# A hybrid decoder block on one core: the opening rebuilt with constant products in its waits, one w_in turn moved, the second norm with one root

## The chip, the core and the metric

The kernel runs on one core of a Trainium2 chip. The metric is the device time of one execution, in microseconds (us). The engines are named as in the profile: PE (matrix products), PEld (its weight loads, which overlap PE), DVE (vector), ACT (scalar), POOL (GpSimd) and SP, whose queue issues nearly all loads here.

## The reference

One decoder block, batch 1, 256 tokens, D = 2048, everything fp32. Cut to what matters:

```python
mod = silu(c) @ w_ada + b_ada                       # c: (1, 2048), w_ada: 2048 x 12288
sh1, sc1, g1, sh2, sc2, g2 = split(mod, 6)
h = rms_norm(x, norm1_g) * (1 + sc1) + sh1
q, k, v, gb, gc, xt = split(h @ w_in, 6)            # w_in: 2048 x 6144
attn = moba_attention(norm(q), norm(k), v)          # 256 tokens: one block, causal
conv = gb * causal_dwconv(gc * xt)
x = x + g1 * (concat(norm(attn), norm(conv)) @ w_out)
h2 = rms_norm(x, norm2_g) * (1 + sc2) + sh2
u_gate, u_up = split(causal_dwconv(h2 @ w_ffn_up), 2)
x = x + g2 * ((silu(u_gate) * u_up) @ w_ffn_down)
```

All inputs are drawn at random; `c` is one row, so each part of `mod` is one vector of 2048 numbers.

## The kernel before

**Precision.** An fp32 product is built from fp32r products of split operands: `hi` is the rounded copy of a weight tile (ACT, L329), `lo` the rest (DVE subtraction, L166, the line of the helper that records all DVE work), and likewise `h` and its residual for the tokens. A product is hi x h, lo x h and hi x residual of h, all into one PSUM bank.

**Slots.** The weights go by in slots: a raw tile of 1 MB is loaded (SP), split into hi on ACT, into lo on DVE, and multiplied on PE. There are six raw buffers (one of them holds partial sums for a while), three hi and three lo. The slots of w_in come in the order of the table `turns`: `['v', 2, 4]` is the pair of column groups v0, v1 on contraction chunks 2 and 3, one slot; `['g1', 4, 8]` is one group on four chunks, one slot. Slot 0 is c, 1 v, 2 g, 3 x, 4 and 5 q, 6 c, 7 and 8 k, 9 g, 10 to 12 x, 13 v; slot 24 is the last slot of `['q0', 4, 16]`. Partial sums leave PSUM when the next slot of the same columns is far: the first time by a copy on ACT (L531), later by an addition on DVE (L166), tiles `pa_...`.

**Banks.** PSUM has eight banks, and `bank()` hands out the one that has been free longest. A slot with a pair takes four (two column groups by two tiles of 128 tokens). Two groups fill the eight; an ada part on PE (below) takes one between them. So slot 3 (x) gets three banks that held v, and as its fourth the first one of g: the first product into it waits for the first eviction of g on ACT, which stands in ACT's queue behind the hi of slot 4.

**adaLN parts ("ada").** `mod` is needed column by column. A part is either multiplied on PE (`pe` true: four column quadrants, weights `crep`, which is silu(c) copied 32 times; L396), or added up on DVE with one scalar_tensor_tensor a chunk (L387, L389). Each part then takes a transpose and a reduction to become columns (`cols`, L453). The table `ada` says [part, first chunk, width, pe, first slot, number of slots over which its tiles are spread]; its tiles share the load queue with the slots. `[1, 4, 512, False, 3, 7]` is the scale for chunks 4 to 7, four tiles.

**Order.** Each engine works through its own list in order; the lists follow from the order in which the Python code, `turns`, `ada` and lists such as `x_first` and `hi_late` emit instructions. Loads are issued on SP in the order in which the tiles are consumed.

**The opening** (L1479 to L1565): x is transposed in 128x128 pieces (L1495, xn) while the sum of squares runs on ACT; the root of the first norm becomes two diagonal tiles n1d, which PE multiplies with ones (n1b, L1509) to get the root along the free axis; xnT = xn times that, on DVE. Beside it run the first ada parts on PE: scale for chunks 0 and 1 (two tiles of 1 MB), then shift. Each is copied out (adae, ACT L417), transposed (adac, L453) and reduced on DVE (adaz). The scaled tokens hf, the shift and the hi of slot 0 give the first product mc (`go_first`, L583: 16 products with hi, 8 with lo).

**The second norm** (`evac_c`, `diag`, L700 to L736): the last w_out column group is added to x, its squares are summed, and the two token tiles get their roots one after the other; n2d, n2b and h2 follow as in the first norm, and the first slots of w_up (`one`, L1042 to L1050) multiply the first h2.

Of the kernel before, what the change touches and what calls it, by code (L numbers as in the profile page):

```python
# [147 lines left out]
def tile_block(  # L148
# [77 lines left out]
    V.tensor_copy(identb, ident)  # L226

# [118 lines left out]
    class Ada:  # L346


        def __init__(self, part, c0, n, pe):
            self.part, self.c0, self.n, self.pe = part, c0, n, pe  # L350
            self.rows = 2048 // n
            self.tiles = NK // self.rows
            self.nch = n // P
            self.acc = None
            self.two = []
            self.used = 0

        def want(self, r):
            a = self.part * D + self.c0 * P
            k0 = r * self.rows  # L360

            def issue(t):
                nc.sync.dma_start(self.view(t), w_ada[0, k0 * P:(k0 + self.rows) * P, a:a + self.n]
                                  .rearrange("(k p) f -> p k f", p=P))
            return issue

# [172 lines left out]
    def pair_load(k, f):  # L539
        def issue(t):  # L540

            n = 1 if not slots_begun else 2
            slots_begun.append(f)
            for j in range(0, 2, n):
                nc.sync.dma_start(t.rearrange("p (k h) f -> p k (h f)", k=2)[:, j:j + n],
                                  w_in[0, (k + j) * P:(k + j + n) * P, COL[f] * 512:COL[f] * 512 + 1024]
                                  .rearrange("(k p) f -> p k f", p=P))
# [152 lines left out]
    def evac_c(f):  # L700
# [7 lines left out]
        def one(t, s, i):  # L708
            V.scalar_tensor_tensor(out=y[t][:, s], in0=g[i][:, :s.stop - s.start], scalar=r[:, t:t + 1], in1=gB[G1, f][:, s],
                                   op0=ALU.mult, op1=ALU.mult)  # L710
            if i == 2:

                V.scalar_tensor_tensor(out=ss2[:, 3, 1:2], in0=q[:, 1:2], scalar=1.0 / D, in1=ss2[:, 3, 1:2],
                                       op0=ALU.mult, op1=ALU.add)
# [316 lines left out]
    def up_slots(grp, ka, kb, one, hold, between=None):  # L1031
        for k in range(ka, kb, 4):
            def go(hi, lo, k=k):
# [9 lines left out]
                if one:  # L1043
                    for j in range(4):
                        for ft in range(4):
                            o, a = zp[grp][ft][:, :256], slice(ft * P, (ft + 1) * P)
                            for w, v in ((hi, 0), (hi, 1), (lo, 0)):
                                mm(o, w[:, j, a], h2T[k + j][:, v * 256:v * 256 + 256],  # L1048
                                   start=begins and j == 0 and w is hi and not v,
                                   stop=ends and j == 3 and w is lo)  # L1050
# [120 lines left out]
    ada_init = [Ada(SC1, 0, 256, True), Ada(SH1, 0, 256, True)]  # L1171

# [331 lines left out]
    ada_init[0].consume(0)  # L1504
    pr = bank("n1b")
# [25 lines left out]

# [3 lines left out]
    parts = [(slice(2 * k, 2 * k + 2), t1k("hf"), t2k(f"h{k}", F32R)) for k in range(2)]  # L1535
    b1 = SH1 * NK
    for k, (s, h, hk) in enumerate(parts):
        hT[k] = halves(hk)
        V.tensor_scalar(h, xnT[0][:, k * 256:(k + 1) * 256], A1[:, k:k + 1], bcol[:, b1 + k:b1 + k + 1],
                        op0=ALU.mult, op1=ALU.add)  # L1540
    s = parts[0][0]
    if CFG["first_hi"]:
        V.tensor_copy(hi[:, s], w[:, s])
    else:
        act(hi[:, s], w[:, s], AF.Copy)
    z, _ = ada_init[1].cols(True)
    for k, (s, h, hk) in enumerate(parts):
        act(hT[k][0], h, AF.Identity, bias=z[:, k:k + 1])
        if not k:
            act(hi[:, parts[1][0]], w[:, parts[1][0]], AF.Copy)  # L1550
    for k, (s, h, hk) in enumerate(parts):
        V.scalar_tensor_tensor(out=hT[k][1], in0=h, scalar=z[:, k:k + 1], in1=hT[k][0].bitcast(F32),
# [106 lines left out]
```

## Time and profile before

| what | us |
|---|---|
| three runs | 1145.74, 1145.96, 1147.56; median 1145.96 |
| the profiled execution | 1145.98 |
| its span (first to last instruction) | 1144.2 |
| PE busy in the span | 1129.7 (99%) |
| DVE busy | 1064.4 (93%) |
| ACT busy | 731.6 (64%) |
| waits of PE for another engine or a load, sum | about 10.8, nearly all before 24 us |

The mean TensorE clock granted in the profiled execution is 0.997 of full speed. A row of the timeline reads: start, duration of the group, engine, line, operation, out<-in, shape, count, and in brackets the idle time of the engine before it with what ended it. A row of the table by windows reads: window, its length, busy time and number of instructions of PE, PEld, DVE, ACT and POOL, then the granted PE clock, the busy share of the DMA engines and the GB/s.

### The profile page before, as it was taken

How to read it: one execution, taken by the hardware profiler on the slowest of the kernel's cores; microseconds unless marked ns; L12 is line 12 of the kernel's file. 1: busy time of each engine (PE TensorE's matmuls, PEld its weight loads, DVE VectorE, ACT ScalarE, POOL GpSimd, SP SyncE). 2: the span in 40 equal slices, each digit the busy share in tenths (PEclk: the TensorE clock that was granted, in tenths of full speed). 3: DMA queues.
4: the chain of work that ended last, by engine and by line, in shares of the span. 5: the costliest groups of instructions: out<-in, count | busy, mean ns of one | idle time of the engine just before them, and what ended most of it. 6: DMA issues, size and time to landing. Idle time of an engine off the chain costs nothing.

```text
span 1144.2 us, 16252 instructions
## 1 busy us (share of the span) xinstructions
PE 1129.7 (99%) x6035; PEld 954.1 (83%) x6035; DVE 1064.4 (93%) x1167; ACT 731.6 (64%) x1091; POOL 61.5 (5%) x90
## 2 busy tenths in 40 slices
PE   6999999999999999999999999999999999999998
PEld 4777778888888879988888888888888888888887
DVE  4789989989999998889999999899999999999798
ACT  4644455576786555566687676776677768866731
POOL 1000000000000000000000000101011101111000
PEclk8999999999999999999999999999999999999999
DMA  9999998998998899987679887999899988999951
GB/s 361 407 412 397 412 371 302 408 382 308 331 397 314 290 317 359 325 278 245 213 246 369 305 293 248 310 360 299 313 272 340 317 317 265 351 313 303 367 222 74
DMA packets 198687, 363.66 MB, mean 318 GB/s; under 512 B 9408, under 2 KB 108180, under 8 KB 194000
## 3 DMA queue, kind: packets, MB, share of 16 engines
q1 hardware_dynamic: 189152, 343.44, 82.8%
q0 software_dynamic: 8160, 17.04, 6.9%
q10 hardware_dynamic: 1296, 2.16, 0.6%
q8 instruction: 47, 0.77, 0.2%
q14 instruction: 32, 0.26, 0.1%
HBM read 343.70 MB, written 18.89 MB: 317 GB/s over the span
## 4 chain that ended last, share of the span: by engine, by line
PE 94%; DVE 2%; DMA 2%; issue 1%; ACT 1%; SPq 0%; DVEq 0%; ACTq 0%
PE z L1063 24%; PE z L1066 13%; PE u L1002 4%; PE u L1004 4%; PE u L1000 4%; PE z L1048 4%; PE ada L396 1%; DVE lo L166 1%; PE mx L516 1%; PE mq L516 1%; PE mg L516 1%; PE mk L516 1%; PE mx L517 1%; PE mv L516 1%; PE mg L517 1%; PE mq L517 1%
## 5 line engine op out<-in xcount | busy, mean ns | idle before, releaser
L329 ACT ACTIVATE hi<-raw 128x2048 fp32r<-128x2048 f32 (+1 forms) x227 | 417.6, 1857 | 263.6 <-DMA raw<-in_w_in_dram 73.5
L166 DVE TENSOR_TENSOR lo<-raw,hi 128x2048 fp32r<-128x2048 f32 (+2 forms) x229 | 501.6, 2200 | 23.3 <-ACT hi L329 23.1
L1063 PE MATMUL z<-h,hi 128*128 128x512 f32 x1280 | 303.3, 390 | 0.3 <-DVE ub L166 0.3
L1063 PEld LDWEIGHTS z<-h,hi 128*128 128x128 f32 x1280 | 237.8, 188 | 49.5 <-ACT hi L329 0.8
L389 DVE SCALAR_TENSOR_TENSOR ada<-raw,csil,ada 128x512 f32<-128x512 f32 (+3 forms) x167 | 195.7, 1175 | 5.3 <-DMA raw<-in_w_ada_dram 1.8
L1066 PEld LDWEIGHTS z<-h,lo 128*128 128x128 f32 x1280 | 163.1, 191 | 5.6
L1066 PE MATMUL z<-h,lo 128*128 128x256 f32 x1280 | 165.0, 283 | 0.0
L1002 PE MATMUL u<-hi,gh 128*128 128x512 f32 x224 | 88.1, 394 | 0.1
L1004 PE MATMUL u<-hi,gl 128*128 128x512 f32 x224 | 87.7, 392 | 0.0
L1000 PE MATMUL u<-lo,gh 128*128 128x512 f32 x224 | 61.4, 390 | 0.0
L812 ACT ACTIVATE uy<-ub,fc,fc 128x256 f32<-128x256 f32 x88 | 47.6, 599 | 11.9 <-DVE ub L166 11.9
L944 POOL DMA_DIRECT2D down_sums<-pu x42 | 36.7, 1290 | 304.3 <-ACT pu L940 304.3
L1002 PEld LDWEIGHTS u<-hi,gh 128*128 128x128 f32 x224 | 42.2, 188 | 10.0 <-ACT pu L940 2.9
L1000 PEld LDWEIGHTS u<-lo,gh 128*128 128x128 f32 x224 | 41.9, 188 | 9.2 <-DVE lo L166 0.3
L1004 PEld LDWEIGHTS u<-hi,gl 128*128 128x128 f32 x224 | 42.2, 189 | 7.5
L1048 PE MATMUL z<-h,hi 128*128 128x256 f32 x256 | 46.6, 284 | 0.4 <-ACT h L771 0.2
L823 ACT ACTIVATE tap<-ub,fc 128x256 f32<-128x256 f32 x96 | 41.7, 504 | 0.0
L1048 PEld LDWEIGHTS z<-h,hi 128*128 128x128 f32 x256 | 40.0, 192 | 0.8 <-ACT h L771 0.5
L166 DVE TENSOR_TENSOR ub<-z,ub 128x256 f32<-128x256 f32 x96 | 33.8, 414 | 7.2 <-ACT ub L844 7.1
L301 DVE TENSOR_TENSOR raw<-raw 128x1024 f32<-128x1024 f32 x32 | 38.9, 1217 | 1.2 <-DMA raw<-in_w_ffn_down_dram 1.2
L844 ACT ACTIVATE ub<-z 128x256 f32<-128x256 f32 x96 | 28.6, 383 | 12.7 <-PE z L1063 12.7
L1048 PE MATMUL z<-h,lo 128*128 128x256 f32 x128 | 36.2, 283 | 0.0
(460 smaller groups left out, 1787.3 us busy)
## 6 DMA issues: line engine op xcount, KB each, us to landing
raw<-in_w_ada_dram SPq DMA_DIRECT2D x96, 1024.0 KB, 7.4
raw<-in_w_ffn_up_dram SPq DMA_DIRECT2D x176, 512.0 KB, 6.1
raw<-in_w_in_dram SPq DMA_DIRECT2D x47, 1024.0 KB, 8.1
raw<-in_w_ffn_down_dram SPq DMA_DIRECT2D x44, 1024.0 KB, 9.5
raw<-in_w_out_dram SPq DMA_DIRECT2D x16, 1024.0 KB, 5.9
raw<-in_w_ffn_down_dram SPq DMA_DIRECT2D x32, 512.0 KB, 4.9
down_sums<-pu POOLq DMA_DIRECT2D x56, 256.0 KB, 8.0
raw<-in_w_ffn_down_dram SPq DMA_DIRECT2D x32, 256.0 KB, 5.3
```

Source lines behind the costliest of these rows:

```text
L166: f(*a, **k)
L329: act(hi[:, :n], t[:, :n], AF.Copy)
L389: W.scalar_tensor_tensor(out=self.acc, in0=t[:, j, :], scalar=csil[:, i:i + 1], in1=self.acc, op0=ALU.mult, op1=ALU.add)
L516: mm(o, a, hi[:, k, s], start=(first and k == 0), stop=False)
L812: act(y[:, s], b[:, s], AF.Identity, bias=bias[:, i + j:i + j + 1], scale=w[2][:, i + j:i + j + 1])
L823: act(z[:, s], b[:, s], AF.Copy, scale=w[2 - d][:, i + j:i + j + 1])
L1000: mm(bank_of(key), a, lo[:, n], start=False, stop=j in ends)
L1002: mm(bank_of(key), a, hi[:, n], start=key not in begun, stop=False)
L1004: mm(bank_of(key), b, hi[:, n], start=False, stop=False)
L1048: mm(o, w[:, j, a], h2T[k + j][:, v * 256:v * 256 + 256], start=begins and j == 0 and w is hi and not v, stop=ends and j == 3 and w is lo)
L1063: mm(zp[grp][ft], hi[:, j, ft * P:(ft + 1) * P], h2T[k + j], start=begins and j == 0, stop=ends and j == 3 and not late)
L1066: mm(zp[grp][ft][:, :256], lo[:, j, ft * P:(ft + 1) * P], h2T[k + j][:, :256], start=False, stop=ends and j == 3 and late)
```

## The change

Five pieces, all in one step.

1. The opening. 34 constant products `onesr` x `onesr` (128x128, result used by nobody) stand between the real PE work. The second shift tile is loaded and multiplied in two halves. The shift's columns come from two products with a 128x1 column `sel` in place of two transposes and a reduction. hf moves ahead on DVE; the first h is made on DVE and the second on ACT; slot 0's load is four DMAs of 128x512, and its hi four pieces, two on ACT and two on DVE.
2. `turns`: v on chunks 2 and 3 goes from slot 13 to slot 7, in front of k; k1, v0, g1 follow each other in a new order.
3. `ada`: the scale for chunks 4 to 7 starts two slots later and is spread over six slots instead of seven.
4. The second norm: the mean squares of both token tiles, one root for both, then both diagonals.
5. The `one` slots of w_up: for each chunk first hi x h for four row tiles, then lo x h, then hi x residual; before, the three came row tile by row tile. `x_first` and `hi_late`, which shift pieces of FFN work by a place, change in some entries.

```diff
-  ..., [1, 4, 512, False, 3, 7], ...
+  ..., [1, 4, 512, False, 5, 6], ...
-       'turns': [['c', 0, 2], ['v', 0, 2], ['g', 0, 2], ['x', 0, 2], ['q', 0, 2], ['q', 2, 4], ['c', 2, 4], ['k', 0, 4],
-                 ['g', 2, 4], ['x', 2, 4], ['x', 4, 8], ['v', 2, 4], ['g1', 4, 8], ['k1', 4, 8], ['v0', 4, 8], ['c', 4, 8],
+       'turns': [['c', 0, 2], ['v', 0, 2], ['g', 0, 2], ['x', 0, 2], ['q', 0, 2], ['q', 2, 4], ['c', 2, 4], ['v', 2, 4],
+                 ['k', 0, 4], ['g', 2, 4], ['x', 2, 4], ['x', 4, 8], ['k1', 4, 8], ['v0', 4, 8], ['g1', 4, 8], ['c', 4, 8],
+       'busy': [9, 4, 5, 5, 5, 6],
+       'norm_at': [4, 8, 8],
...
+    V.tensor_reduce(out=sel, in_=ident.rearrange("p (j r) -> p j r", j=4)[:, :, 0], axis=AX.X, op=ALU.add)
...
+    def keep_busy(b, n):
+        for _ in range(n):
+            mm(b[:, 256:384], onesr, onesr, start=True, stop=True)
...
-    xn_norm(0, 1, 2, 3)
-    ada_init[0].consume(1)
-    ada_init[0].evac()
-    ada_init[0].cols()
-    xn_norm(4)
+    xn_norm(*range(n0))
+    sc.consume(1)
+    keep_busy(p_one, w1)
+    sc.evac()
+    sc.cols()
+    hf = []
+    b1 = SH1 * NK
+    for k in range(2):
+        hf.append(t1k("hf"))
+        V.tensor_scalar(hf[k], xnT[0][:, k * 256:(k + 1) * 256], A1[:, k:k + 1], bcol[:, b1 + k:b1 + k + 1],
+                        op0=ALU.mult, op1=ALU.add)
+    xn_norm(*range(n0, 5))
     xn_tr(5)
-    ada_init[1].consume(0)
+    keep_busy(p_one, w2)
+    sh.products(0, 0, 8)
     xn_tr(6, 7)
-    xn_norm(5, 6, 7)
-    ada_init[1].consume(1)
-    ada_init[1].evac()
+    keep_busy(p_one, w3)
+    xn_norm(*range(5, n1))
+    sh.products(1, 0, 4)
+    sh.products(1, 4, 8)
+    keep_busy(p_one, w4)
+    rows_sum = t2k("adae")[:, :256]
+    act(rows_sum, sh.acc, AF.Copy)
+    for k in range(2):
+        mm(p_one[:, k:k + 1], rows_sum[:, k * P:(k + 1) * P], sel, start=k == 0, stop=k == 1)
+    keep_busy(bank("two"), w5)
+    z = small(8, "adaz")[:, :2]
+    V.tensor_copy(z, p_one[:, :2])
...
+    act(hi[:, 0], w[:, 0], AF.Copy)
+    for k in range(2):
+        hT[k] = halves(hk[k])
+        if k:
+            act(hT[k][0], hf[k], AF.Identity, bias=z[:, k:k + 1])
+        else:
+            V.tensor_scalar(hT[k][0], hf[k], z[:, k:k + 1], None, op0=ALU.add)
+    rest(0)
+    V.tensor_copy(hi[:, 1], w[:, 1])
+    rest(1)
+    act(hi[:, 2], w[:, 2], AF.Copy)
+    V.tensor_copy(hi[:, 3], w[:, 3])
...
         one(0, slice(0, 512), 0)
         one(1, slice(0, 256), 1)
-        root(0, 0)
         one(1, slice(256, 512), 2)
         nrm["p"] = bank("n2b")
-        diag(0)
-        root(1, 2)
-        diag(1)
+        add(0, 0, m)
+        add(1, 1, ss2[:, 3])
+        add(1, 2, m)
+        g, r = nrm["t"][:, :2], nrm["r"][:, :2]
+        act(g, m[:, :2], AF.Sqrt)
+        rsqrt_b(r, m[:, :2], g)
+        for t in range(2):
+            nrm["d", t] = t1k("n2d")[:, :P]
+            V.tensor_scalar(nrm["d", t], ident, r[:, t:t + 1], None, op0=ALU.mult)
...
-                        for ft in range(4):
-                            o, a = zp[grp][ft][:, :256], slice(ft * P, (ft + 1) * P)
-                            for w, v in ((hi, 0), (hi, 1), (lo, 0)):
+                        for w, v in ((hi, 0), (lo, 0), (hi, 1)):
+                            for ft in range(4):
+                                o, a = zp[grp][ft][:, :256], slice(ft * P, (ft + 1) * P)
```

**The opening on PE.** Before, from the scale's second tile to the first product of slot 0 (n1b is the root, ada_0_165 the scale, ada_0_219 the shift, adac their transposes, xn the pieces of x):

```order
L1509 MATMUL n1b<-n1d,ones 128x128 x2
L396 MATMUL ada_0_165<-raw,crep 32x256 x8
L453 MATMUL adac_0_206<-ident,adae_0_203 128x128 x2
L1495 MATMUL xn_214<-ident,xr 128x128 x4
L396 MATMUL ada_0_219<-raw,crep 32x256 x8
L1495 MATMUL xn_230<-ident,xr 128x128 x2
L1495 MATMUL xn_233<-ident,xr 128x128 x2
L1495 MATMUL xn_230<-ident,xr 128x128 x2
L1495 MATMUL xn_233<-ident,xr 128x128 x2
L396 MATMUL ada_0_219<-raw,crep 32x256 x8
L453 MATMUL adac_0_268<-ident,adae_0_256 128x128 x2
L583 MATMUL mc_293<-hi,h_261 128x512
```

Now, the last part of the same stretch, from the shift's first tile on:

```order
L1526 MATMUL one<-onesr 128x128 x5
L381 MATMUL ada_0_247<-raw,crep 32x256 x8
L1513 MATMUL xn_258<-ident,xr 128x128 x2
L1513 MATMUL xn_261<-ident,xr 128x128 x2
L1513 MATMUL xn_258<-ident,xr 128x128 x2
L1513 MATMUL xn_261<-ident,xr 128x128 x2
L1526 MATMUL one<-onesr 128x128 x5
L381 MATMUL ada_0_247<-raw,crep 32x256 x8
L1526 MATMUL one<-onesr 128x128 x5
L1571 MATMUL one<-sel,adae 128x1 x2
L1526 MATMUL two<-onesr 128x128 x6
L606 MATMUL mc_335<-hi,h_309 128x512
```

Each real group now has five or six constant products before it (nine stand before n1b, four before the scale's adac), and the two transposes of the shift have become two products of one column.

**Loads on SP and ada work on DVE, slots 4 to 10.** Before, the SP queue from the load of slot 4 (w_in tiles are slots, w_ada tiles of 128x4x512 belong to the scale for chunks 4 to 7 or to the shift for the same chunks):

```order
L545 DMA raw<-in_w_in_dram 128x2x1024
L363 DMA raw<-in_w_ada_dram 128x4x512
L545 DMA raw<-in_w_in_dram 128x2x1024
L363 DMA raw<-in_w_ada_dram 128x4x512 x2
L545 DMA raw<-in_w_in_dram 128x2x1024 x2
L363 DMA raw<-in_w_ada_dram 128x4x512 x2
L545 DMA raw<-in_w_in_dram 128x2x1024 x2
L363 DMA raw<-in_w_ada_dram 128x4x512 x3
```

Now, from the same load on:

```order
L568 DMA raw<-in_w_in_dram 128x2x1024 x2
L369 DMA raw<-in_w_ada_dram 128x4x512
L568 DMA raw<-in_w_in_dram 128x2x1024 x2
L369 DMA raw<-in_w_ada_dram 128x4x512 x3
L568 DMA raw<-in_w_in_dram 128x2x1024 x2
L369 DMA raw<-in_w_ada_dram 128x4x512 x3
L568 DMA raw<-in_w_in_dram 128x2x1024
```

Slot 4's load keeps its place; the loads of slots 5, 8 and 9 stand one place earlier, those of 6 and 7 two; everything ahead of slot 4 has as many bytes as before. On DVE, now, v's evictions (pa_v) after slot 7, with the ada tiles around them:

```order
L168 TENSOR_TENSOR lo<-raw,hi 128x2048
L168 TENSOR_TENSOR pa_v_427<-mv_700,pa_v_427 128x512
L168 TENSOR_TENSOR pa_v_429<-mv_701,pa_v_429 128x512
L168 TENSOR_TENSOR pa_v_431<-mv_714,pa_v_431 128x512
L168 TENSOR_TENSOR pa_v_433<-mv_715,pa_v_433 128x512
L409 SCALAR_TENSOR_TENSOR ada_4_639<-raw,csil,ada_4_639 128x512 x4
L168 TENSOR_TENSOR lo<-raw,hi 128x2048
```

Before, no eviction of v stood here: v1's two tiles (pa_v is one tile for each column group and token tile) went after slot 13, v0's two after slot 16, v1's two again after slot 20. Now it is four tiles here, then v0's two and v1's two: eight before slot 24 where six were.

**The first products of w_up on PE.** Before (z_0 to z_3 are the four row tiles; in each `x2` the first is hi x h, the second hi x residual):

```order
L1048 MATMUL z_0_3762<-h_0_3702,hi 128x256 x2
L1048 MATMUL z_0_3762<-h_0_3702,lo 128x256
L1048 MATMUL z_1_3763<-h_0_3702,hi 128x256 x2
L1048 MATMUL z_1_3763<-h_0_3702,lo 128x256
L1048 MATMUL z_2_3764<-h_0_3702,hi 128x256 x2
```

Now:

```order
L1065 MATMUL z_0_3803<-h_0_3743,hi 128x256
L1065 MATMUL z_1_3804<-h_0_3743,hi 128x256
L1065 MATMUL z_2_3805<-h_0_3743,hi 128x256
L1065 MATMUL z_3_3806<-h_0_3743,hi 128x256
L1065 MATMUL z_0_3803<-h_0_3743,lo 128x256
L1065 MATMUL z_1_3804<-h_0_3743,lo 128x256
L1065 MATMUL z_2_3805<-h_0_3743,lo 128x256
L1065 MATMUL z_3_3806<-h_0_3743,lo 128x256
L1065 MATMUL z_0_3803<-h_0_3743,hi 128x256
```

The residual of h was the second operand asked for; it is the ninth now.

More of the change, by code (lines that the diff above doesn't have):

```diff
@@ L356, in __init__ @@
             self.used = 0
+            self.cuts = {}
         def want(self, r):
@@ L362, in issue, with products @@
             def issue(t):
-                nc.sync.dma_start(self.view(t), w_ada[0, k0 * P:(k0 + self.rows) * P, a:a + self.n]
-                                  .rearrange("(k p) f -> p k f", p=P))
-            return issue
+                for i, j in self.cuts.get(r, [(0, self.rows)]):
+                    nc.sync.dma_start(self.view(t)[:, i:j], w_ada[0, (k0 + i) * P:(k0 + j) * P, a:a + self.n]
+                                      .rearrange("(k p) f -> p k f", p=P))
+            return issue
+        def products(self, r, i, j):
+            if i == 0:
+                self.used += 1
+                self.held = self.view(take((self, r)))
+            if self.acc is None:
+                self.acc = bank(f"ada{self.part}_{self.c0}")[:, :self.n]
+            for k in range(i, j):
+                q = 32 * (k % 4)
+                mm(self.acc[q:q + 32, :], crep[:, self.rows * r + k, :], self.held[:, k, :],
+                   start=r == 0 and k < 4, stop=r == self.tiles - 1 and k >= self.rows - 4,
+                   tile_position=(0, q))
+            if j == self.rows:
+                load_next()
         def home(self):
@@ L540, in issue @@
         def issue(t):
[L542 to L547, printed above, removed]
+            if not slots_begun:
+                slots_begun.append(f)
+                for j in range(4):
+                    a = (COL[f] + j % 2) * 512
+                    nc.sync.dma_start(t[:, j], w_in[0, (k + j // 2) * P:(k + j // 2 + 1) * P, a:a + 512])
+                return
+            nc.sync.dma_start(t.rearrange("p (k h) f -> p k (h f)", k=2),
+                              w_in[0, k * P:(k + 2) * P, COL[f] * 512:COL[f] * 512 + 1024]
+                              .rearrange("(k p) f -> p k f", p=P))
         return issue
@@ L1504, in tile_block @@
     ada_init[0].consume(0)
+    def keep_busy(b, n):
+        for _ in range(n):
+            mm(b[:, 256:384], onesr, onesr, start=True, stop=True)
+    p_one = bank("one")
+    w0, w1, w2, w3, w4, w5 = CFG["busy"]
+    keep_busy(p_one, w0)
     pr = bank("n1b")
@@ L1554, in tile_block, with rest @@
-    for s, _, _ in parts:
-        V.tensor_tensor(out=lo[:, s], in0=w[:, s], in1=hi[:, s].bitcast(F32), op=ALU.subtract)
+    done.update((SH1, k) for k in range(2))
+    hk = [t2k(f"h{k}", F32R) for k in range(2)]
+    act(hi[:, 0], w[:, 0], AF.Copy)
[5 more added lines that the diff above has]
+            V.tensor_scalar(hT[k][0], hf[k], z[:, k:k + 1], None, op0=ALU.add)
+    def rest(k):
+        V.scalar_tensor_tensor(out=hT[k][1], in0=hf[k], scalar=z[:, k:k + 1], in1=hT[k][0].bitcast(F32),
+                               op0=ALU.add, op1=ALU.subtract)
@@ L1556, in tile_block @@
+    rest(0)
[3 more added lines that the diff above has]
+    V.tensor_copy(hi[:, 3], w[:, 3])
+    xn_norm(*range(n1, n2))
+    for j in range(0, 4, 2):
+        V.tensor_tensor(out=lo[:, j:j + 2], in0=w[:, j:j + 2], in1=hi[:, j:j + 2].bitcast(F32), op=ALU.subtract)
+    xn_norm(*range(n2, 8))
     splits.append((hi, lo))
```

45 lines of the change are left out of this document (11 added, 34 removed), and 2 rows, old and new, of the table CFG.

## The prediction

> **What bounds the kernel now.** I read the page first, for busy time and the shares of the chain of waits, then the view of PE's waits.
>
> ```profile
> PE 1129.7 (99%) x6035; PEld 954.1 (83%) x6035; DVE 1064.4 (93%) x1167; ACT 731.6 (64%) x1091; POOL 61.5 (5%) x90
> ...
> PE 94%; DVE 2%; DMA 2%; issue 1%; ACT 1%; SPq 0%; DVEq 0%; ACTq 0%
> ...
> PE n1b L1509 <- DVE n1d L166: 1.1, 1, 1.1
> PE mc L583 <- ACT h L1548: 1.1, 1, 1.1
> PE adac L453 <- ACT adae L417: 1.0, 2, 0.5
> PE ada L396 <- DMA raw<-in_w_ada_dram: 0.7, 1, 0.7
> ...
> PE z L1048 <- ACT h L771: 0.2, 1, 0.2
> ```
>
> PE is the bound: 99% busy, 94% of the chain. What it still waits for in the part that is rebuilt is 1.1 + 1.1 + 1.0 + 0.7 = 3.9 us, and 0.2 in the second norm. The rest of a gain can only come from the PE clock, so the second view is the table by windows of 3.41 us in the opening.
>
> ```profile
> 11.01:14.43 3.42, 1.60 (x21) 0.81 (x19) 1.30 (x7) 2.08 (x5) 2.35 (x5) 1.00 1.09 385
> 14.43:17.84 3.41, 2.96 (x20) 1.40 (x20) 1.86 (x4) 0.77 (x2) 0.00 (x0) 0.50 1.09 379
> 17.84:21.25 3.41, 3.35 (x42) 2.27 (x46) 2.85 (x9) 0.00 (x1) 0.00 (x0) 1.00 1.06 416
> 21.25:24.67 3.42, 1.83 (x17) 0.86 (x10) 2.46 (x7) 1.79 (x4) 0.00 (x0) 1.00 1.02 414
> 24.67:28.08 3.41, 3.41 (x9) 2.65 (x8) 2.84 (x4) 2.35 (x3) 0.00 (x0) 0.50 1.03 399
> ```
>
> The column before the last two is the granted PE clock: two windows run at half speed, and each follows a window in which PE was busy for only 1.60 or 1.83 us; after 2.96 us and more the next one is full. So filling the waits should lift both. The third thing to read, further down, is how long before PE asks for them tiles and banks stand ready: that decides what is left of a gain.
>
> **The opening up to slot 1.** Rows of the chain of waits (start, duration, what):
>
> ```profile
> 15.53 1.91 PE ada L396 x16
> ...
> 17.89 0.44 PE adac L453 x2
> 18.33 0.44 PE xn L1495 x4
> 18.77 1.00 PE ada L396 x16
> ...
> 23.82 7.41 PE mc L583 x24
> 31.23 0.23 PE mv L516
> ```
>
> and of the timeline:
>
> ```profile
> 21.82 0.73 DVE L166 TENSOR_SCALAR hf<-xnT,A,vbc 128x256 f32<-128x256 f32 x2
> 21.86 0.38 ACT L417 ACTIVATE adae<-ada 128x256 f32<-128x256 f32 x1 [4.02 <-PE ada L396]
> 25.55 4.74 DVE L166 TENSOR_TENSOR lo<-raw,hi 128x1024 fp32r<-128x1024 f32 x3
> 32.88 1.07 PE L514 MATMUL mv<-lo,h 128*128 128x512 f32 x4
> ```
>
> The same 16 ada products take 1.91 us at half speed and 1.00 at full. The 24 products of slot 0 take 7.41; at the 0.23 of a full-speed one they take 5.5: 1.9 less. Between the end of the shift's second tile (21.8) and mc (23.82) lie 2.0 us: the copy 0.38, two transposes 0.44, then hf and hi on DVE in front of the reduction, then h on ACT. Now hf is done earlier and hi stands behind; what is left is the copy 0.38, two one-column products (none in the trace; at most the 0.44 of two transposes, at least nothing; I take 0.4, since the 128x128 weights are loaded for them all the same), a small DVE copy (0.16, the kind of the 128x2 operations) and one h on DVE (0.36, half of the hf row), some 0.2 for hand-overs: 1.5, so 0.5 less. The shift's second tile may start as soon as half of it has landed, with less half-speed work ahead of it: between nothing and the 0.7 that PE once waited for such a load; I take 0.2. Sum: slot 1 starts 1.9 + 0.5 + 0.2 = 2.6 us earlier than 31.07, capped by slot 1's lo: it ends at 25.55 + 4.74 = 30.29 whatever PE does (its load sets it), and PE asks for it at 32.88, so 2.6 is also the most. The constant products have no row. The nearest are transposes of the same size, 0.44 for four: 34 x 0.11 = 3.7 us at full speed, which the 3.9 us of waits hold; at half speed 7.4, of which 3.5 would stand in front of real work. I take the first.
>
> **What is left of these 2.6 us: two places.** The first is slot 3. By the allocation of banks told above, its fourth bank is the first one of g, and PE's first product there waits for g's first eviction. Three rows of the timeline and one by windows:
>
> ```profile
> 44.33 1.92 ACT L329 ACTIVATE hi<-raw 128x2048 fp32r<-128x2048 f32 x1 [4.04 <-DMA raw<-in_w_in_dram]
> 46.15 2.04 ACT L531 ACTIVATE pa_g<-mg 128x512 f32<-128x512 f32 x4
> ...
> 47.65 0.39 PE L516 MATMUL mx<-hi,h 128*128 128x512 f32 x1
> ```
>
> ```profile
> 31.50:50.00 18.50, 18.50 (x104) 13.84 (x103) 14.73 (x22) 9.55 (x15) 0.00 (x0) 1.00 1.05 406
> ```
>
> ACT is idle for 4.04 us until slot 4's load lands, makes its hi, and only then evicts g; the first of the four evictions ends at 46.15 + 0.51 = 46.7. PE comes to that bank at 47.65. So the reserve is 0.95 us. The load cannot come earlier: the DMA share is 1.05 from the opening on (the same in the windows above), the bytes ahead of it are the same and so is its place, and the order on ACT is unchanged. PE, 2.6 us early, waits there until it is 0.95 early. This holds for anything between 0.95 and 2.6, so it makes the sum nearly independent of how well the clock is lifted.
>
> The second is slot 24. A row by windows, four of the timeline, and two of DVE's waits between 38 and 94 us:
>
> ```profile
> 94.05:164.39 70.34, 70.34 (x330) 54.55 (x329) 69.59 (x70) 27.89 (x40) 0.00 (x0) 1.00 1.03 400
> ```
>
> ```profile
> 159.36 1.28 DVE L166 TENSOR_TENSOR pa_v<-mv,pa_v 128x512 f32<-128x512 f32 x2
> ...
> 163.15 1.09 ACT L1180 ACTIVATE hf<-xnT,B,A 128x256 f32<-128x256 f32 x2 [0.93 <-DVE B L166]
> ...
> 169.76 5.51 ACT L329 ACTIVATE hi<-raw 128x2048 fp32r<-128x2048 f32 x3
> ...
> 171.77 0.45 PE L516 MATMUL mq<-hi,h 128*128 128x512 f32 x1
> ```
>
> ```profile
> DVE lo L166 <- ACT hi L329: 7.4, 6, 2.1
> ...
> DVE ada L389 <- DMA raw<-in_w_ada_dram: 1.8, 2, 1.4
> ```
>
> Its hi is the first of three on ACT, 169.76 + 1.9 = 171.66, and PE takes it at 171.77: 0.11 in reserve. That hi stands behind the h tiles, these behind DVE's B, and DVE is busy for 69.59 of the 70.34 us before. So a gain passes slot 24 only as far as DVE comes out of this stretch earlier, and that depends on DVE's own work and idle time, not on PE. The 1.8 us for ada loads are two, both for tiles of the scale for chunks 4 to 7; the new order asks for w_in first and gives DVE these tiles two slots later, landed, so I count them as gone. The waits for hi are pinned by landings: 5 of 6 loads come one or two places earlier, but DVE then also has less to do between them, so I leave their 7.4 as it is. Against that stand two evictions of v more before slot 24 (eight for six), at 1.28 / 2 less overlap = 0.61 each: 1.2. Net 0.6 earlier, and with the 0.11 of reserve PE is 0.7 us earlier behind slot 24. Ends: 0.95, the bank in slot 3; and 1.1 later than before if the 1.8 come back as other waits and the evictions remain (1.2 - 0.11). I take 0.7: it is worked from rows, and both parts stand in the lists of DVE.
>
> **The second norm and w_up**, in the timeline:
>
> ```profile
> 423.17 0.15 DVE L166 SCALAR_TENSOR_TENSOR n2m<-n2q,ss 128x1 f32<-128x1 f32 x1
> ...
> 424.37 0.29 DVE L166 TENSOR_SCALAR n2d<-ident,n2r 128x128 f32<-128x128 f32 x1
> ...
> 426.30 0.88 DVE L166 SCALAR_TENSOR_TENSOR h<-h2f,B,h 128x256 fp32r<-128x256 f32 x2 [0.18 <-ACT h L771]
> 426.32 0.90 PE L1048 MATMUL z<-h,hi 128*128 128x256 f32 x2 [0.24 <-ACT h L771]
> 427.18 0.40 PE L1048 MATMUL z<-h,hi 128*128 128x256 f32 x2
> ```
>
> The second tile's mean at 423.17 came behind the first tile's root on DVE; with one root it comes some 0.3 earlier, but now the first tile's diagonal (0.29) stands behind the root too: 0.1 gained, 0 to 0.3. The first two z products take 0.90 us where a later pair takes 0.40: the second one waits for the residual of h (426.30, DVE). With the new order eight products stand between, so 0.4 is gained, 0.1 to 0.5 if the next chunk's h becomes the wait. Sum 0.45. `x_first`, `hi_late` and the swap of k1, v0, g1 move work where PE shows no wait of over 0.3 us; nothing, plus or minus 0.3.
>
> **Sum.** The profiled execution took 1145.98 us (span 1144.2, 1.8 outside it, unchanged), 0.02 above the median. 1145.98 - 0.7 - 0.45 = **1144.8**. A measurement of this kernel can tell 0.2%, 2.3 us, from no change (the runs before lie 1.8 apart), so this is "the same".
>
> **Rivals.**
> *The bank and DVE don't hold it.* If slot 4's load lands 1.5 us earlier, or DVE comes out as early as PE, the 2.6 stay: 1145.98 - 2.5 - 0.45 = 1143.0. For it: PE's waits before show neither limit, since it was later than both. Against: DMA at 1.05, DVE at 69.59 of 70.34. 15%.
> *The clock isn't lifted.* The first constants add at most nine to a window with 1.60 us busy: 1.60 + 9 x 0.11 = 2.6, and where between 1.83 and 2.96 the clock changes is unknown. With both windows at half speed only the shorter chain remains, 0.5 or less at slot 1, and at slot 24 between 0.11 and 0.5: 1145.98 - 0.4 - 0.45 = 1145.1. One window alone leaves over 0.95 and changes nothing. 11%. [...]
> *DVE later.* v's evictions come, the 1.8 us return as other waits: slot 24 is 1.1 later, 1145.98 + 1.1 - 0.45 = 1146.6. For it: DVE has no slack after 94 us. It decides when DVE's waits between 38 and 94 us still sum up to what they are now. 10%.
> *The constants themselves in the way, at half speed.* PE works them in order, so at half speed 3.5 us of them stand before real work, 0.5 comes back from the shorter chain, and slot 1 starts 3.0 later; slot 3's reserve doesn't help a late PE. 1145.98 + 3.0 - 0.45 = 1148.5. It needs two half-speed windows in a row from 14.43 on; against it, 2.96 busy us released the clock at 17.84. 6%.
>
> **Chances.** The forecast has 56%, its own range 1143.6 to 1145.6, one tenth of it below 1143.67 (0.2% under the median); 2% are left for anything else. Faster by over 0.2%: 0.13 of the first rival, 0.06 of the forecast, 0.01: 0.20. Slower: 0.05 of the last, 0.02 of others: 0.07. Same: 0.73. The range reaches from just above the first rival to DVE later: 1143.6 to 1146.7.
>
> **What would show it.** Right: no half-speed window after 14.4; slot 1 near 28.5; a wait of some 1.5 us at slot 3's fourth bank with ACT's copy of g as its end; DVE without a wait for ada loads between 60 and 90 us; PE waiting at slot 24 for hi at about 171.0. Wrong: slot 24's hi before 170.5 or after 171.7, a half-speed window, a PE wait between 24 and 420 us that isn't one of these, or z's second product still 0.5 us behind its first.

## The result: slower by 7 us, with slower weight loads

| | us |
|---|---|
| before, six runs beside the change | 1145.95 median (1145.18 to 1147.56) |
| after, six runs | 1152.98 median (1152.0 to 1156.21) |
| ratio after / before | 1.0061, 95% interval 1.0049 to 1.0073 |
| the profiled execution of after | 1154.48, span 1152.7 |

The forecast was 1144.8 in a range of 1143.6 to 1146.7. The time lies 6 us above the range.

The page of after, in its parts on busy time, the chain, the queues and the loads (kind, count, KB each, median us from issue to landing):

```profile
PE 1134.1 (98%) x6071; PEld 956.2 (83%) x6071; DVE 1066.2 (92%) x1168; ACT 730.3 (63%) x1090; POOL 61.3 (5%) x90
...
q1 hardware_dynamic: 189456, 343.44, 84.2%
...
PE 71%; DMA 12%; DVE 10%; ACT 3%; issue 2%; SPq 0%; DVEq 0%; ACTq 0%
...
raw<-in_w_ada_dram SPq DMA_DIRECT2D x95, 1024.0 KB, 8.2
...
raw<-in_w_in_dram SPq DMA_DIRECT2D x47, 1024.0 KB, 10.3
raw<-in_w_out_dram SPq DMA_DIRECT2D x16, 1024.0 KB, 7.7
```

The same rows of the page of before that the prediction did not quote:

```profile
q1 hardware_dynamic: 189152, 343.44, 82.8%
...
raw<-in_w_ada_dram SPq DMA_DIRECT2D x96, 1024.0 KB, 7.4
...
raw<-in_w_in_dram SPq DMA_DIRECT2D x47, 1024.0 KB, 8.1
raw<-in_w_out_dram SPq DMA_DIRECT2D x16, 1024.0 KB, 5.9
```

PE fell from 94% of the chain to 71%, and DMA rose from 2% to 12%. The bytes are the same (343.44 MB), the packets took longer: share times 16 engines times span over packets is 80.1 ns a packet before and 82.0 after. Loads of equal size land later in all three groups. ACT's and DVE's own work on the raw tiles is no slower: `hi<-raw` takes 1857 ns before and 1858 after, `lo<-raw,hi` 2200 in both pages.

The windows of the opening show where this begins. After:

```profile
11.01:14.43 3.42, 2.72 (x29) 2.02 (x29) 1.14 (x6) 1.38 (x2) 1.73 (x4) 1.00 1.09 346
14.43:17.84 3.41, 2.96 (x31) 2.18 (x31) 2.88 (x8) 0.77 (x2) 0.00 (x0) 1.00 1.11 341
17.84:21.25 3.41, 3.29 (x45) 2.33 (x45) 3.22 (x6) 0.00 (x0) 0.00 (x0) 1.00 1.09 362
...
24.67:28.08 3.41, 3.41 (x17) 2.82 (x16) 2.69 (x3) 0.81 (x2) 0.00 (x0) 1.00 1.01 401
```

Read the last three columns against the windows of before in the prediction. The PE clock is 1.00 where it was 0.50, as was forecast (whether the constants did this is taken up below). But at the same DMA share (1.09 and 1.11 against 1.09) the load engines move 346 and 341 GB/s, not 385 and 379: a tenth less for the same busy time.

What that does to PE, in the timeline of after:

```profile
29.40 0.50 PE L536 MATMUL mv<-hi,h 128*128 128x512 f32 x1 [0.28 <-ACT hi L333]
...
47.27 1.92 ACT L333 ACTIVATE hi<-raw 128x2048 fp32r<-128x2048 f32 x1 [4.68 <-DMA raw<-in_w_in_dram]
...
49.72 0.50 PE L536 MATMUL mx<-hi,h 128*128 128x512 f32 x1 [0.58 <-ACT pa_g L551]
...
176.22 0.50 PE L536 MATMUL mq<-hi,h 128*128 128x512 f32 x1 [0.54 <-ACT hi L333]
...
430.99 0.74 PE L1065 MATMUL z<-h,hi 128*128 128x256 f32 x4 [0.24 <-ACT h L788]
```

Against the same places before (31.07, 44.33, 47.65, 171.77, 426.32): slot 1 starts 1.7 earlier. Slot 4's load, whose landing starts that hi, comes 2.9 later. So slot 3's fourth bank is 2.1 later, slot 24 4.5 later, and the first product of w_up 4.7 later. The wait for the copy of g at the fourth bank is there as predicted; it was the time of the load that was not.

The two profiled executions differ by 8.5 us in their spans (1152.7 and 1144.2). Set side by side product by product, counted from the end of PE's list, PE is 4.3 us late at 640 us, 6.2 at 760, 7.0 at 890 and 8.0 at 1050. So about half of the loss stands in front of the FFN, and the rest arises at a few places in it, to which the third group comes back.

### The profile page after: what moved, and what is told of

Same layout as the page of the kernel before. It is cut to its first block, busy times and chain, and to the rows that moved or that the text cites. A ratio compares the mean times of both kernels' runs of the same rounds, so it can differ in the third digit from the quotient of the medians.

```text
span 1152.7 us, 16328 instructions
## 1 busy us (share of the span) xinstructions
PE 1134.1 (98%) x6071; PEld 956.2 (83%) x6071; DVE 1066.2 (92%) x1168; ACT 730.3 (63%) x1090; POOL 61.3 (5%) x90
## 3 DMA queue, kind: packets, MB, share of 16 engines
q1 hardware_dynamic: 189456, 343.44, 84.2%
## 4 chain that ended last, share of the span: by engine, by line
PE 71%; DMA 12%; DVE 10%; ACT 3%; issue 2%; SPq 0%; DVEq 0%; ACTq 0%
PE z L1080 23%; PE z L1083 12%; DMA raw<-in_w_in_dram 7%; DVE lo L168 5%; PE z L1065 4%; PE u L1017 4%; PE u L1019 3%; PE u L1021 3%; DMA raw<-in_w_ffn_down_dram 2%; DMA raw<-in_w_ada_dram 2%; DVE ada L409 2%; ACT hi L333 2%; DMA raw<-in_w_ffn_up_dram 1%; PE mx L536 1%; PE mg L536 1%
## 5 line engine op out<-in xcount | busy, mean ns | idle before, releaser
L333 ACT ACTIVATE hi<-raw 128x2048 fp32r<-128x2048 f32 (+1 forms) x227 | 418.2, 1858 | 272.0 <-DMA raw<-in_w_in_dram 65.7
L1080 PEld LDWEIGHTS z<-h,hi 128*128 128x128 f32 x1280 | 237.9, 188 | 49.5 <-ACT hi L333 0.8
L1083 PE MATMUL z<-h,lo 128*128 128x256 f32 x1280 | 165.2, 283 | 0.0
L1065 PE MATMUL z<-h,hi 128*128 128x256 f32 x256 | 36.4, 284 | 0.2 <-ACT h L788 0.2
L168 DVE TENSOR_TENSOR uy<-tap,uy 128x510 f32<-128x510 f32 (+1 forms) x48 | 32.8, 684 | 2.0 <-ACT tap L840 0.2
L168 DVE SCALAR_TENSOR_TENSOR uy<-ub,fc,uy 128x254 f32<-128x254 f32 (+1 forms) x80 | 33.6, 476 | 0.6
```

The costliest lines, as they stand in the source:

```text
L168: f(*a, **k)
L333: act(hi[:, :n], t[:, :n], AF.Copy)
L1065: mm(o, w[:, j, a], h2T[k + j][:, v * 256:v * 256 + 256], start=begins and j == 0 and w is hi and not v, stop=ends and j == 3 and v == 1)
L1080: mm(zp[grp][ft], hi[:, j, ft * P:(ft + 1) * P], h2T[k + j], start=begins and j == 0, stop=ends and j == 3 and not late)
L1083: mm(zp[grp][ft][:, :256], lo[:, j, ft * P:(ft + 1) * P], h2T[k + j][:, :256], start=False, stop=ends and j == 3 and late)
```

## The experiments

The first group undid one part of the change at a time; the second tested the cause that its traces pointed to; the third asked which tiles it is, and tried the prediction's own steps without it. None leaves a part of the computation out.

### First group: one part undone at a time

No constants (`no_const`):

```diff
-       'busy': [9, 4, 5, 5, 5, 6],
+       'busy': [0, 0, 0, 0, 0, 0],
```

> The changed kernel without its 34 constant products, all else as changed. If the constant products (or the full PE clock that they bring) slow the loads, packets of 1 KB go back from 51 ns to 46 in the opening and the time to 1146 or less. If the loads are slow for another reason, two windows of the opening run at half speed again, packets stay at 50 to 51 ns, slot 4's load stays at about 47.2 us, and the time stays between 1152 and 1155, since PE waits for loads anyway.

The opening's loads as before, slot 0 in two DMAs and the shift's second tile in one (`old_loads`):

```diff
-    ada_init[1].cuts[1] = [(0, 4), (4, 8)]
...
-                for j in range(4):
-                    a = (COL[f] + j % 2) * 512
-                    nc.sync.dma_start(t[:, j], w_in[0, (k + j // 2) * P:(k + j // 2 + 1) * P, a:a + 512])
+                for j in range(2):
+                    nc.sync.dma_start(t.rearrange("p (k h) f -> p k (h f)", k=2)[:, j:j + 1],
+                                      w_in[0, (k + j) * P:(k + j + 1) * P, COL[f] * 512:COL[f] * 512 + 1024]
+                                      .rearrange("(k p) f -> p k f", p=P))
```

> The changed kernel with the loads of before in the opening: the shift's second tile in one DMA, slot 0 in two DMAs of 128x1024. If the split loads bring the slow packets, 46 ns and about 1145 (the 1144.8 of the prediction). If not, 1152 to 1155 and packets at 50 to 51 ns.

The turns and the `ada` row as before (`old_turns`): the two `-` rows of these tables in the change's diff put back.

> The changed kernel with the order of slots and the start of the scale for chunks 4 to 7 as before. The loads after 40 us then come in the order of before; the packets before 40 us were slow already, so if they cause the loss, little comes back: 1151 to 1154. If the moved turn of v (two evictions more on DVE) causes it, 1146 to 1148.

And the kernel before once more (`before_again`), unchanged:

> The kernel before once more, for its packets and landings on the chip of these runs. If the slow packets belong to a chip or a session, it shows 50 ns too and about 1152; if they belong to the changed kernel, 46 ns and 1145 to 1147.6.

| kernel | us, median | ratio to before, interval | GB/s, 14.43 to 17.84 us |
|---|---|---|---|
| `no_const` | 1151.95 | 1.0048, 1.0031 to 1.0066 | 341 |
| `old_loads` | 1153.79 | 1.0062, 1.0043 to 1.0081 | 341 |
| `old_turns` | 1152.32 | 1.0054, 1.0034 to 1.0075 | 343 |
| `before_again` | 1148.42, one execution | | 382 |

Whatever was undone, the time stayed at 1152 to 1154 and the loads stayed slow: the cause is none of these three parts alone. Without constants one window at half speed came back (0.52, from 24.67 to 28.08 us) where two were expected, and slot 4's hi still starts at 46.95 (47.27 in after); the loads move 341 and 361 GB/s from 14.43 to 21.25 us (341 and 362 in after), so the constants don't slow the loads. `before_again` missed its expectation of 1145 to 1147.6, but its loads are as fast as before, so the slow loads belong to the changed kernel; its extra time arises at about 750 us, in the FFN.

Among what the three still share with after, and not with before, is the column `sel`. It is a tile of 4 bytes in each partition, which takes 32, and it is allocated ahead of all large tiles. With it, the raw tiles start at byte 30240 of a partition, where they started at 30208 = 59 x 512; hi moves from 87552 to 87584, lo from 114176 to 114208. (From 30208 to 87552 it is seven raw buffers of 8192 bytes; the description of the kernel above says six.)

### Second group: is it the 32 bytes?

The change in full with the old places (`aligned`): two later 8-byte tiles share one, which makes room for `sel`.

```diff
-        r = const.tile([P, 2], F32, name="r" + w)
+        if not rAC:
+            rAC["both"] = const.tile([P, 4], F32, name="rAC")
+        r = rAC["both"][:, :2] if w == "A" else rAC["both"][:, 2:]
```

> The change in full, but the two 8-byte tiles of the attention and convolution norms share one padded tile of 32 bytes, so that with the new column sel the raw, hi and lo tiles start where they start before the change (raw at byte 30208 of a partition, hi at 87552, lo at 114176) and not 32 bytes behind. Nothing else differs from the change. Placement theory (loads are slower in the changed kernel because every tile that a load writes starts 32 bytes off): the loads in the opening come back to 380 to 415 GB/s where the changed kernel has 341 to 362, slot 4's load lands near 44.3 us and not at 47.2, and the time is that of the prediction, 1144.8, between 1143.0 and 1146.7. Rival (something else that the change adds slows the loads: a new instruction, another order of the DMAs): 1151 to 1155, loads as slow as in the changed kernel.

The kernel before with 32 bytes too many (`before_32`):

```diff
     V.tensor_copy(identb, ident)
+    pad = const.tile([P, 1], F32, name="pad")
+    V.tensor_copy(pad, ident[:, :1])
```

> The kernel before with one more constant tile of 4 bytes (padded to 32), written once and read by nobody, at the place where the change puts sel: all raw, hi and lo tiles 32 bytes later, no other difference. Placement theory: all of the loss and none of the change, so 6 to 9 us over before: 1152 to 1155; 341 to 362 GB/s in the opening where the kernel before has 379 to 416. Rival (something else in the change): 1146, as before.

Two other distances (`sel_64` and, with 64 columns in place of 16, `sel_256`):

```diff
-    sel = const.tile([P, 1], F32, name="sel")
+    sel = const.tile([P, 16], F32, name="sel")[:, :1]
```

> The change in full with sel in a tile of 64 bytes, so that the raw tiles start 64 bytes behind their old place (64 modulo 512) and not 32. Three readings of the placement theory. If only starts off a multiple of 64 cost, this is 1144.8 (1143 to 1146.7). If starts off a multiple of 256 or 512 cost, it is 1151 to 1155 like the changed kernel. If the cost grows with the offset, it is slower than 1154. [...] Rival (placement has nothing to do with it): 1151 to 1155.

> The change in full with sel in a tile of 256 bytes: the raw tiles start 256 bytes behind their old place (256 modulo 512). If starts off a multiple of 64 or of 256 cost, this one is 1144.8 (1143 to 1146.7); if only multiples of 512 are clean, 1151 to 1155. [...] Rival (placement has nothing to do with it): 1151 to 1155.

| kernel | raw starts at, mod 512 | GB/s, 14.43 to 17.84 us | us, median | ratio to before, interval |
|---|---|---|---|---|
| before | 0 | 379 | 1146.09 | |
| `before_32` | 32 | 341 | 1153.07 | 1.0059, 1.0045 to 1.0073 |
| after | 32 | 341 | 1152.98 | 1.0061, 1.0049 to 1.0073 |
| `sel_64` | 64 | 341 | 1152.85 | 1.0061, 1.0047 to 1.0075 |
| `sel_256` | 256 | 380 | 1145.73 | 0.9997, 0.9988 to 1.0006 |
| `aligned` | 0 | 381 | 1145.73 | 0.9998, 0.9989 to 1.0007 |

The placement accounts for the whole loss. The kernel before with 4 idle bytes more is as slow as the change, and the change in its old place is as fast as before. 64 bytes cost what 32 do, 256 cost nothing: of the four distances tried, the multiples of 256 are free (128 was not tried). Why a load into such a start takes longer, no run shows.

The packets in the traces show the size of it. Between 14.43 and 17.84 us all packets of the load queue but 16 or 17 of 4 bytes are of 1 KB, and their median is 46 ns in before and 51 in after (starts at 0 and at 32). With a start at 256 the share and the rate are those of before (1.09 and 380 GB/s), with one at 64 nearly those of after (1.10 and 341). Between 31.5 and 50 us a packet of 2 KB takes 84 ns in before and 87 in after, one of 4 KB 159 and 164. So in these stretches a packet takes 3 to 5 ns more at each of the three sizes, which is most where packets are small.

The page, the windows and the timeline of `before_32`, to set beside those of before:

```profile
q1 hardware_dynamic: 189152, 343.44, 84.5%
```

```profile
14.43:17.84 3.41, 1.98 (x23) 1.06 (x22) 2.85 (x8) 0.77 (x2) 0.00 (x0) 1.00 1.10 341
...
31.50:50.00 18.50, 16.20 (x91) 11.39 (x90) 13.05 (x20) 9.08 (x14) 0.00 (x0) 1.00 1.06 378
```

```profile
47.05 1.92 ACT L331 ACTIVATE hi<-raw 128x2048 fp32r<-128x2048 f32 x1 [4.68 <-DMA raw<-in_w_in_dram]
```

With none of the change in it, slot 4's hi starts at 47.05 (44.33 before) and PE, which was busy for all of the 18.50 us after 31.5, is idle for 2.3 of them. A packet takes 82.1 ns on average. In its profiled execution PE is 5.1 us late by 250 us, and the FFN adds nothing to that (4.8 at the end).

### Third group: which tiles, and the prediction's steps without the shift

Only the raw tiles in their old place, and everything behind them (hi, which x is loaded into, lo, partial sums, work tiles) 32 bytes later (`others_32`); the diff is against `aligned`:

```diff
     xr = []
+    pad = sb.tile([P, 8], F32, tag="pad", bufs=1, name="pad")
+    nc.gpsimd.memset(pad, 0.0)
```

> The aligned version with a tile of 32 bytes between the raw tiles and the rest: raw starts at byte 30208 as before the change, but hi (which x is loaded into), lo, the partial sums and all work tiles start 32 bytes later, as in the changed kernel. If what costs is the place that the weight loads write to: 1144.5 to 1147, 380 to 415 GB/s in the opening, as in the aligned version. Rival (what costs is the place that the engines read and write: hi, lo and the work tiles off a multiple of 256): 1151 to 1155. A share in both: between.

It took 1145.98 (0.9998, 0.9989 to 1.0007). Its windows and its timeline:

```profile
14.43:17.84 3.41, 3.41 (x25) 2.15 (x24) 1.11 (x2) 0.39 (x1) 0.00 (x0) 1.00 1.10 382
```

```profile
13.13 2.19 PE L1530 MATMUL one<-onesr 128*128 128x128 f32 x9
...
16.21 1.94 PE L416 MATMUL ada<-raw,crep 128*32 128x256 f32 x16
...
30.99 0.39 PE L536 MATMUL mv<-hi,h 128*128 128x512 f32 x1
```

So it is the raw tiles, the ones that the weight loads write, and not the other tiles. The raw tiles are also read, by ACT and DVE, but that takes as long in after as in before (the 1858 and 2200 ns above).

In this execution the first products ran at half speed: 2.19 us for nine constants and 1.94 for sixteen ada products, where `aligned` took 1.22 and 1.07. The clock column says 1.00 there all the same. The clock records of this trace begin only at 18.3 us, and where a trace has no record the column shows 1.00 (in before, too, from 7.60 to 11.01 us, with the first record at 11.01). Slot 1 started at 30.99; what that cost is said below.

The prediction's steps, each undone in `aligned`. Without constants (`aligned_no_const`, the diff of `no_const`):

> The aligned version without the 34 constant products. Prediction's second step (slot 3's fourth bank caps the gain, so the time hardly depends on the clock in the opening): one or two half-speed windows come back before 28.1 us, slot 1 starts 1 to 2 us later than the aligned version's 27.9, PE's wait for the first copy of g shrinks or goes, and behind slot 3 PE is at most 0.5 later than in the aligned version: 1145.5 to 1146.3. Rival (no cap: the gain of the opening reaches the end): 1 to 2 us over the aligned version, 1146.9 to 1147.7. Second rival (the constants do nothing, windows at full speed without them too): 1145.7, with slot 1 where the aligned version has it.

With the old turns and `ada` row (`aligned_old_turns`):

> The aligned version with the order of the w_in turns, and the slots of the scale for chunks 4 to 7, as before the change. Prediction's third step (slot 24's hi stands behind DVE's work before 94 us): DVE's two waits for ada loads, 1.8 us, come back and two evictions of v, 1.2, go; slot 24's hi ends some 0.6 later than in the aligned version (170.2), between 170.4 and 171.7, and PE behind slot 24 is 0 to 0.9 us later: 1145.7 to 1146.6. Rival (DVE comes out of the opening earlier by itself, so the turns decide nothing): hi at 170.2 or before, PE unchanged at slot 24, 1145.7. The times will hardly tell these apart, the places of hi and of PE in the trace will.

With the old second norm and order of the first products of w_up (`aligned_old_norm`): `evac_c`, `diag` and the loop under `if one` as in the `-` lines of the change.

> The aligned version with the second norm and the order of the first products of w_up as before the change. Prediction's last step: 0.45 us lost between 417 and 432 us (PE's lead over the kernel before falls back from about 1.5 to about 1.05 there) and kept to the end: 1146.2. Rival (PE's lead is given back in the FFN whatever the norm does): the same loss at 430, none at the end, 1145.7. In time alone the two are within what can be told; the trace tells them by PE's place at 440 and at 990 us.

| kernel | us, median of 11 | ratio to before, interval |
|---|---|---|
| `aligned` | 1145.73 | 0.9998, 0.9989 to 1.0007 |
| `aligned_no_const` | 1145.54 | 0.9996, 0.9988 to 1.0005 |
| `aligned_old_turns` | 1147.41 | 1.0012, 1.0003 to 1.0021 |
| `aligned_old_norm` | 1146.93 | 1.0005, 0.9996 to 1.0014 |

First the timeline of `aligned`, where the steps can be read undisturbed:

```profile
27.86 0.39 PE L536 MATMUL mv<-hi,h 128*128 128x512 f32 x1
...
44.01 1.92 ACT L333 ACTIVATE hi<-raw 128x2048 fp32r<-128x2048 f32 x1 [4.10 <-DMA raw<-in_w_in_dram]
45.84 2.04 ACT L551 ACTIVATE pa_g<-mg 128x512 f32<-128x512 f32 x4
...
46.46 0.51 PE L536 MATMUL mx<-hi,h 128*128 128x512 f32 x1 [0.48 <-ACT pa_g L551]
...
168.32 5.52 ACT L333 ACTIVATE hi<-raw 128x2048 fp32r<-128x2048 f32 x3
...
170.72 0.39 PE L536 MATMUL mq<-hi,h 128*128 128x512 f32 x1
...
425.17 0.74 PE L1065 MATMUL z<-h,hi 128*128 128x256 f32 x4 [0.24 <-ACT h L788]
```

PE's lead over before is 3.2 us at slot 1 (27.86 against 31.07), 1.2 at slot 3's fourth bank (46.46 against 47.65) and 1.05 at slot 24 (170.72 against 171.77). Slot 4's load landed 0.3 earlier than before and g's first copy with it; the rest of the lead ended in the wait of 0.48 at the bank and one of 0.43 for an ada load just ahead of it.

Without constants one window runs at 0.60 (windows of `aligned_no_const`), slot 1 starts 1.25 later, and behind the bank it is all level again (its timeline):

```profile
21.25:24.67 3.42, 2.69 (x6) 2.15 (x7) 3.05 (x7) 1.14 (x2) 0.00 (x0) 0.60 1.04 419
```

```profile
46.57 0.50 PE L536 MATMUL mx<-hi,h 128*128 128x512 f32 x1 [0.50 <-ACT pa_g L551]
```

46.57 against 46.46. The expectation holds but for one part: the wait for g's copy did not shrink (0.50 for 0.48). By the medians, 1145.73 with the constants and 1145.54 without, the 34 constant products are worth nothing that can be measured in the time.

What an early slot 1 is worth can be read in the profiled execution of `others_32`. Its slot 1 is 3.1 us later than in `aligned`, its first product into the fourth bank 1.1 later (47.58, without a wait), the first product of w_up 0.7 later (425.84). So of 3.1 us some 0.7 is left at w_up. (That execution took 1147.50 and the one of `aligned` 1145.67; most of this difference arises at about 750 us.)

With the old turns, DVE's waits (between 38 and 94 us) and the timeline of `aligned_old_turns`:

```profile
DVE ada L409 <- DMA raw<-in_w_ada_dram: 2.0, 2, 1.4
```

```profile
169.04 5.51 ACT L333 ACTIVATE hi<-raw 128x2048 fp32r<-128x2048 f32 x3
...
171.03 0.46 PE L536 MATMUL mq<-hi,h 128*128 128x512 f32 x1
```

DVE's two ada waits are back (2.0; none in `aligned`), and the hi of slot 24 starts 0.72 later (the prediction's net 0.6). The first of the three hi ends at 169.04 + 1.84 = 170.9, just ahead of PE, which does not wait for it. PE's 0.31 at this slot is not hi's doing: PE is as late from 120 us on. So what the prediction said of hi holds, but this hi holds PE up by 0.13 at most: PE is 0.44 late behind the slot, and 0.18 from 250 us to w_up. The median lies above the expected 1145.7 to 1146.6. `aligned` and this kernel were measured beside different runs of before (medians 1146.09 and 1146.24), so the ratios are to be compared: 0.9998 and 1.0012, with intervals that overlap. In the profiled executions (1145.67 and 1148.67) nearly all of the difference arises in the FFN.

With the old norm, the timeline of `aligned_old_norm`:

```profile
425.08 0.91 PE L1071 MATMUL z<-h,hi 128*128 128x256 f32 x2 [0.24 <-ACT h L794]
425.83 0.28 PE L1071 MATMUL z<-h,lo 128*128 128x256 f32 x1
```

The stall behind z's first product is back (0.91 for two; four take 0.74 in the new order), and PE is 0.32 later than in `aligned` at 437 us. The norm itself brings nothing: z starts at 425.08 with two roots, at 425.17 with one. Again the median, 1146.93, holds more than the step (1146.2 was expected), and the intervals overlap. At 990 us PE is 2.5 later than in `aligned`, by other losses in the FFN, so whether the 0.32 is kept can't be read there.

Where the rest arises can be seen. DVE's waits between 700 and 1000 us in `aligned_old_norm`, then PE's waits in the whole of it:

```profile
DVE raw L305 <- DMA raw<-in_w_ffn_down_dram: 4.8, 3, 2.0
```

```profile
PE u L1027 <- DVE gl L168: 1.3, 2, 0.8
...
PE u L1023 <- DVE lo L168: 0.6, 2, 0.3
```

DVE waits for late loads of w_ffn_down (4.8 us here, 4.9 with the old turns, 2.1 in `aligned`, 1.2 in before), and PE then waits for DVE's gl and lo at about 751 and 880 us. The same is in the profiled executions of `before_again` (4.3 us, beside its 1148.42), of `others_32` (3.3, beside 1147.50) and of after (5.0). So it is not tied to one kernel, and it may be behind much of the spread of 1144 to 1150 of the kernels with raw in its old place. No run undid it, so this is read from the traces and not shown. Whether the two undone steps make it more frequent, or whether chance did, these runs do not settle.

## Why the prediction was wrong, point by point

**The step that failed** is in the part on slot 3: "The load cannot come earlier: the DMA share is 1.05 from the opening on ..., the bytes ahead of it are the same and so is its place". The prediction asked only whether the load could come earlier. Its place in the queue and its bytes are indeed unchanged, but the time of every load was taken from before, and it rose: 341 for 379 GB/s at the same share, slot 4's hi 47.27 for 44.33. The prediction costed `sel` by its two products and put its 32 bytes of memory, ahead of all large tiles, at nothing without a reason. `before_32` shows that these alone cost 7.0 us (1.0059). No rival named it either: the one on the slower side with the highest time, 1148.5, lay in the constants.

**The clock**: right for after, where no half-speed window is left behind 14.4 us. But the rule behind it, that a window with little PE work brings half speed in the next, does not hold. The windows of `before_again`, the same program as before, and two of `before_32`:

```profile
11.01:14.43 3.42, 2.00 (x28) 1.25 (x32) 1.13 (x6) 1.44 (x3) 1.62 (x4) 1.00 1.09 383
14.43:17.84 3.41, 2.48 (x38) 1.32 (x30) 3.14 (x8) 0.56 (x2) 0.00 (x0) 1.00 1.09 382
...
24.67:28.08 3.41, 3.41 (x14) 2.64 (x15) 3.25 (x4) 1.92 (x1) 0.00 (x0) 1.00 1.04 398
```

```profile
11.01:14.43 3.42, 1.72 (x20) 1.02 (x20) 1.19 (x7) 1.49 (x2) 1.75 (x4) 1.00 1.10 345
14.43:17.84 3.41, 1.98 (x23) 1.06 (x22) 2.85 (x8) 0.77 (x2) 0.00 (x0) 1.00 1.10 341
```

No window of either is at half speed, without any constants and with PE busy for only 1.72 to 2.48 us in four of them. In `before_again` slot 1 started at 28.55, 2.5 earlier than in the other execution of the same program: what the constants are to bring, the kernel before has in some executions by itself. Here too the lead was down to 0.65 by 62 us. Of the five traces without constants three fall back to half speed in the opening (before, `no_const`, `aligned_no_const`) and two don't. Of the nine with constants none falls back, but in three (`old_loads`, `old_turns`, `others_32`) the first products run at half speed until after 18 us, and slot 1 starts at 31.0 to 31.3, no earlier than before. What decides it the runs do not show.

**Slot 1 near 28.5**: 27.86 in `aligned`, which is 3.2 earlier than before and more than the 2.6 called the most. The cap was slot 1's lo, set by its load, and in `aligned` that load came 0.4 earlier itself (hi at 25.66 for 26.05), and PE reached the lo products 2.9 early (29.96 for 32.88). In after it is 29.40, where slot 1's own hi was late (0.28 of wait).

**The cap at slot 3**: right. ACT's copy of g is what PE waits for there in after, in `aligned` and in `aligned_no_const`; the wait is 0.5 to 0.6, not 1.5, since an ada load takes the other part of the lead ahead of it. The lead that is left is 1.2 where 0.95 was forecast.

**Slot 24**: the size was off, and 170.2 is outside the bounds (170.5 to 171.7) that the prediction set itself. hi was forecast for 171.0, and in `aligned` the first ends at 170.2. DVE comes out of an early opening earlier by itself, which was not in the sum: with the opening late (`others_32`, same turns) these hi start at 169.29, 0.97 later than in `aligned`. So this place takes nothing away; the lead behind it is 1.05, not 0.7. The two parts, 1.8 of ada waits and 1.2 of evictions, net 0.6, are 0.72 by `aligned_old_turns`. In neither kernel did PE wait there.

**The second norm and w_up**: z's order 0.4 forecast, 0.32 measured; the single root 0.1 forecast, nothing measured.

**The sum**: without the shift the forecast of 1144.8 would stand against 1145.73 (0.9998, 0.9989 to 1.0007 of before, or 1144.8 to 1146.9). That holds it at the very edge. PE's lead in `aligned` is 1.15 at the first product of w_up (425.17 against 426.32), and with the 0.32 of z's order 1.5 behind it, more than the 1.15 forecast for the two steps together; but only 0.3 us of it is left in the span of the profiled execution (1143.9 against 1144.2). The forecast took it that what PE has gained by 430 us stays to the end. Product by product, the lead is 1.6 at 640 us, 1.3 at 950 and 0.8 behind a product at 989 us that waits for DVE's gl; the last 0.5 goes behind PE's last product. DVE waits longer for w_ffn_down there than before (2.1 us and 1.2), but that this is the cause was not tested.

**The rivals**: the first sum takes off 2.5 where its text has 2.6. None of the four accounts for the loss.

## What to carry to other kernels

A new tile, however small, can move everything that is allocated behind it (here 4 bytes moved the raw tiles by 32, and that cost 7.0 us): compare the start addresses of the tiles that loads write before and after a change, and keep them at multiples of 256 bytes, as the free ones here were. In the profile the sign here was about the same DMA share (1.11 for 1.09) with fewer GB/s (341 for 379) and the same bytes (343.44 MB), in a kernel whose own rows look as planned. And where a later wait caps the start (here a bank that an eviction frees behind a load), work on the opening buys little (of 3.2 us at slot 1, 1.2 at the bank): look for that place before rebuilding it.

## What the runs showed of the hardware that was not expected

Loads into tiles that start 32 or 64 bytes off a multiple of 256 moved a tenth less between 14.43 and 17.84 us, where the DMA share is 1.09 to 1.11 (341 for 379 to 382 GB/s). Over the whole kernel a packet took 82.1 ns (`before_32`) for 80.1. A start 256 bytes off the old place cost nothing (380 GB/s). An offset of 32 bytes in the tiles that only engines, and the loads of x, touch cost nothing that can be measured (1145.98). And the granted clock column shows 1.00 also where the trace has no clock record: sixteen ada products took 1.94 us in such a window (`others_32`, before 18.3 us), 1.07 in `aligned`. There the products' own times have to be read.
